# Block 0 of a streaming encoder layer: gate weights and a third conv tap inside the attention, two affine passes on ScalarE, a shorter inverse root

## The chip, the cores and the metric

The kernel runs on one core of one Trainium2 chip. A core has TensorE (PE in the profile: matrix products; its weight loads are shown as PEld), VectorE (DVE), ScalarE (ACT), GpSimd (POOL) and SyncE (SP, which only issues DMAs here). The metric is the device time of one execution in microseconds; a median of several runs is given. Lower is better.

## What is computed

One layer, on 2048 prompt frames and 32 sample frames of width 1024, all in float32:

```
mod = c @ w_mod + b_mod;  shift, scale, gate = split(mod, 3)
h = rms_norm(x, g_pre) * (1 + scale) + shift
a, b, z_conv, q, k, v, z_attn, g_conv, g_attn = split(h @ w_in)      # 512 wide, the last two 1024
u = a * sigmoid(b)
y = causal depthwise conv of u, 31 taps, + dw_b
y_conv = (silu(layer_norm(y)) * silu(z_conv)) @ w_conv_out
o = attention over the own 64-frame chunk and the 8 before it, 8 heads of 64, with a position bias
y_attn = (o * silu(z_attn)) @ w_attn_out
merged = sigmoid(g_conv) * y_conv + sigmoid(g_attn) * y_attn
out = x + gate * rms_norm(merged @ w_o, g_post)
```

The prompt and the sample frames have different conditioning vectors c, so `mod` has two rows. Caches of keys, values and conv inputs go in and out.

## The kernel before, in words

**Precision.** A float32 value is split into a high half (rounded to the type of fast matmuls, `F32R`) and a low half, the remainder. A product is three matmuls: high by high, high by low, low by high (`mm3`, line 257).

**Weights.** All weights of the program stand in one list, `plan` (lines 184 to 200), in the order of use. A call of `weights(key)` takes the next one. It also splits the weight two places ahead (`w_parts`, line 218: ACT rounds the high half, DVE or POOL subtracts), and issues the load of the one four places ahead (`w_load`). Raw weights have two buffers, split ones three. Each entry is 512 KB raw. Most weights are kept split in DRAM (`w_keep`, issued on ACT's queue) and read back by blocks 1 to 3; the gate's weights are used once. Which engine subtracts is chosen by line 227; inside block 0's attention it is POOL for all but gate weights, and in the tail of block 0 (`pace.dense`) it is DVE.

**Blocks and stages.** The frames go in four blocks of 512; block 0 also holds the 32 sample frames, so its projections run as two pieces of 272 columns. A block has these stages:
- value projection; in block 0 it is woven into the start (norm of x, first two thirds of `mod`, and `h`). `h_part` (line 334) makes `h` from a transposed piece: ACT writes the high half, DVE computes the same affine value again in full precision (`hf`), and DVE subtracts.
- attention: units (head pair, head, group of queries) with scores, exponentials, normalisation, transposes and the product with the values. Between these pieces `fill` issues pieces of other projections, in the order that `FILL(b)` gives: gated conv input (b, a), queries and keys of later head pairs, gates (z, c).
- tail: the two 1024-wide gates (`C_GC`, `C_GA`) and the attention branch's output, column by column; then the conv branch's output and the merge (line 1334 on), with `h` of the next block; then `w_o`, the next block's conv input, the post norm and the store.

**The conv** is 31 multiply-adds (taps) on each of 4 channel tiles, 128x574 in block 0, each one DVE instruction (`conv`, line 487). It is a generator that opens when the first channel tile of u is done. In the attention of block 0 it is advanced a fixed number of times at three places of a turn, by `TP`, in all turns but the last three (21 of 24). Otherwise, and in the whole tail, it is advanced when the planner's count for DVE has fallen behind. After the last tap comes `norm_conv` (mean and variance by matmul with a matrix of ones, the inverse root by `rsqrt` on 128x544, then POOL multiplies), and then `co` (line 1237), which makes swish and gate and splits the result into `cohi` and `colo`; the conv branch's product can't start before.

**The planner.** The order on PE, DVE, ACT and POOL is written by the program. `Pace` keeps two clocks, `pe` and `dve`, in estimated us: a matmul adds 6 + 0.4063 ns a column, a DVE instruction by its width (`Vec.call`, line 125). `pace.start(gen, delay)` runs a generator's pieces when `pe` has passed their due time. So `norm_conv`'s pieces are spaced by `YL` and `co`'s by 1.0. SP's queue is ordered by the framework's own scheduler. Three PSUM buffers (`pp`) serve all projections and short products; a projection's drain is issued late, at the next piece or at `pace.flush()`.

**The gate.** The last third of `mod` needs 8 weights (1024 rows by 1024 columns, as 256x512 pieces). Before, `gate_rows` in the tail took one of them after each column of the gates but the first, and the rest behind the last; `gate_row` adds the bias, multiplies by `g_post` and stores to DRAM (`gp_d`), from which the last stage reads it broadcast:

```
for m in (m2, m2 + 1):                       # tail, line 1298
    pace.run(proj(C_GC + m * P, b, ...))
    pace.run(proj(C_GA + m * P, b, ...))
    if gr and m:
        for i in range(2):
            next(gr, None)                   # four gate matmuls in two steps
            pace.tick()
```

Of the kernel before, what the change touches and what calls it, by code (L numbers as in the profile page):

```python
# [8 lines left out]
F32 = mybir.dt.float32  # L9
# [7 lines left out]
P = 128  # L17
D = 1024
# [16 lines left out]
NIN = 5632  # L35
BIG = 1e30
# [9 lines left out]
TP = (1, 1, 0)  # L46
# [5 lines left out]
def FILL(b):  # L52

    part = dict(q=C_Q, k=C_K, a=C_A, b=C_B, z=C_ZA, c=C_ZC)
# [84 lines left out]
def mixer_kernel(ctx, tc, x_prompt, x_sample, c_prompt, c_sample, cache_conv, cache_k, cache_v,  # L139
# [78 lines left out]
    def w_parts(i):  # L218

        if i < len(plan):  # L220
            key = plan[i][0]
            w = wp.tile([P, 2, 1024], F32R, tag="w", name="w", bufs=3)
            wh, wl = w[:, 0], w[:, 1]
            if i <= keep_at[key]:
                raw = raws.pop(i)
                act(wh, raw, AF.Copy)  # L226
                on_v = key[0] == "mod" or pace.dense or pace.idle is None and pace.dve <= pace.pe + DV
                (V if on_v else G).tensor_tensor(wl, raw, wh.bitcast(F32), op=OP.subtract)  # L228
            else:
                nc.sync.dma_start(w.bitcast(F32), kept[key])  # L230
            halves[i] = w
# [83 lines left out]
    def h_stats(pool, b, xs):  # L315

        xs += load_x(pool, b)
        yield 8.0
        ss = pool.tile([P, 8], F32, tag="ss", name="ss", bufs=2)
        V.memset(ss, 1.0)  # L320
        for t, (xt, m) in enumerate(xs):
            junk = ps.tile([P, 1024], F32, tag="S", name="junk")
            act(junk[0:m], xt[0:m], AF.Square, accum_out=ss[0:m, t:t + 1])
# [4 lines left out]
        V.tensor_scalar(ss, ss, 1.0 / D, EPS, op0=OP.mult, op1=OP.add)  # L328
# [152 lines left out]
    conv_ready, ln_done = set(), {}  # L481
# [78 lines left out]
    def mod_rows(n, dst):  # L560
        pm = ps.tile([P, 512], F32, tag="T", name="pm", bufs=2)
        for kp in range(KT // 2):
            wh, wl = weights(("mod", 2 * kp, n * 512))
            for kk in range(2):
                k = 2 * kp + kk
                mm(pm[0:4], c4[:, k, :], wh[:, kk, :], k == 0, False)
                mm(pm[0:4], c4[:, k, :], wl[:, kk, :], False, k == KT - 1)
                yield
        V.tensor_copy(dst, pm[0:4])

    def gate_rows(tmp):

        for n in range(2):
            m4, bg = tmp("m4")[0:4, 0:512], tmp("bg")
            bm, gr = bg[0:2, 0:512], bg[0:2, 512:1024]
            nc.sync.dma_start(bm, dram(b_mod, 2 * D + n * 512, [[0, 2], [1, 512]]))
            nc.sync.dma_start(gr, dram(g_post, n * 512, [[0, 2], [1, 512]]))
            yield from mod_rows(4 + n, m4)
            pace.start(gate_row(n, m4, bm, gr), 4.0)

    def gate_row(n, m4, bm, gr):
        pg = pp_tile("pg")
        nc.tensor.matmul(pg[0:2], lhsT=sel, rhs=m4, start=True, stop=True)
        V.tensor_tensor(bm, pg[0:2], bm, op=OP.add)
        V.tensor_tensor(bm, bm, gr, op=OP.mult)
        nc.sync.dma_start(gp_d[:, n * 512:(n + 1) * 512], bm)
        yield 0.0
# [31 lines left out]
    with tc.tile_pool(name="init", bufs=1) as ini:  # L619
# [64 lines left out]
        with tc.tile_pool(name="x0", bufs=5) as x0:  # L684
# [37 lines left out]
            V.tensor_scalar(ss, ss, 1.0 / D, EPS, op0=OP.mult, op1=OP.add)  # L722
# [74 lines left out]
    for b in range(NB):  # L797
# [5 lines left out]
        with tc.tile_pool(name="at", bufs=1) as at:  # L803
# [136 lines left out]
            def z_proj(col, dst, key):  # L940
                def sink(o, c0, c1):
                    tz = tmp("tz")
                    act(tz[:, c0:c1], o, AF.Tanh, scale=0.5)
                    V.scalar_tensor_tensor(dst[:, c0:c1], tz[:, c0:c1], 1.0, o, op0=OP.add, op1=OP.mult)
                def done():
# [5 lines left out]
                    C_B: lambda n: b_proj(b, n), C_A: lambda n: a_proj(b, n, tmp),  # L951
                    C_ZA: lambda n: z_proj(C_ZA + n * P, aof[:, n], ("za", n)),
# [225 lines left out]
            rate = (88.0 if b == 0 else 62.0) / sum(loads)  # L1178
# [50 lines left out]
        with tc.tile_pool(name="tl", bufs=1) as tl_:  # L1229
# [7 lines left out]
            def co():  # L1237
# [5 lines left out]
                def first(ct):  # L1243
                    xn[ct] = tl_.tile([P, NT], F32, tag="t1", name="xn", bufs=2)
                    th[ct] = tl_.tile([P, NT], F32, tag="hf", name="th", bufs=2)
                    for a0, a1, o0 in ypieces:
# [3 lines left out]
                        V.tensor_scalar(xn[ct][:, o0:o1], Y[ct][:, a0:a1], vecs[:, 44 + ct:45 + ct],  # L1250
                                        vecs[:, 48 + ct:49 + ct], op0=OP.mult, op1=OP.add)
# [42 lines left out]
            gr = gate_rows(lambda name: tl_.tile([P, D], F32, tag="x", name=name, bufs=XB)) if b == 0 else None  # L1294
            for m2 in range(0, KT, 2):
                if m2 == KT - 4 and b < NB - 1:
                    pace.start(h_stats(XP, b + 1, xs))
                for m in (m2, m2 + 1):
# [4 lines left out]
                    if gr and m:  # L1303
                        for i in range(2):
                            next(gr, None)
                            pace.tick()
# [59 lines left out]
            def gated(t, n):  # L1366
# [5 lines left out]
                act(jk[0:m], acc[t][0:m], AF.Square, accum_out=sq[0:m, n * 8 + t:n * 8 + t + 1])  # L1372
# [3 lines left out]
            def store(t0, t1, parts, apart=()):  # L1376
# [3 lines left out]
                V.tensor_scalar(rx[:, c], rx[:, c], 1.0 / D, EPS, op0=OP.mult, op1=OP.add)  # L1380
# [63 lines left out]
```

## Time and profile before

| | |
|---|---|
| median of 3 runs | 1776.56 us (1776.23 to 1776.82) |
| the profiled execution | 1774.66 us |
| its span, first to last instruction | 1772.9 us |
| mean granted TensorE clock | 0.982 |
| DVE busy | 1154.7 us (65%) |
| ACT busy | 597.5 us (34%) |
| POOL busy | 212.1 us (12%) |

Busy times are sums over the span. PE's matmuls are pipelined and their ends modelled, so a busy PE is not PE at its peak; idle time of PE is the surer reading. Block 0 takes about the first 632 us; blocks 1 and 2 some 400 each.

### The profile page before, as it was taken

What the parts mean: (1) busy time and instruction counts of PE and PEld (TensorE: products, weight loads), DVE (VectorE), ACT (ScalarE), POOL (GpSimd) and SP (SyncE); (2) the same over time, 40 slices, a digit from 0 to 9 for tenths busy, and PEclk for the clock granted to TensorE, in tenths of its full rate; (3) what the DMA queues carried; (4) which work ended last, traced back from release to release, by engine and by line L of the source; (5) the groups of instructions that cost most, each with busy time, mean ns of one, the idle gap of its engine ahead of it and who ended that gap; (6) DMA issues with size and microseconds to landing.
All of it is one profiled execution on the core that took longest, in us unless ns stands there. A gap on an engine that the chain in (4) does not pass through costs nothing.

```text
span 1772.9 us, 23618 instructions
## 1 busy us (share of the span) xinstructions
PE 1690.7 (95%) x9221; PEld 1430.4 (81%) x9221; DVE 1154.7 (65%) x2119; ACT 597.5 (34%) x1156; POOL 212.1 (12%) x163
## 2 busy tenths in 40 slices
PE   6889999989499999999899999999999999999997
PEld 4778899988388788888788888888888888888886
DVE  6556876887855957775652967765652967766523
ACT  5345454233331245531220035531320045531211
POOL 4322222002220000001120000001120000000120
PEclk9999999999699999999999999999999999999999
DMA  8796565767375684465465585455565574445553
GB/s 267 216 326 207 189 215 202 272 229 262 132 255 196 243 305 174 156 221 190 150 217 188 196 307 188 140 198 210 181 218 191 199 272 144 171 167 201 190 190 143
DMA packets 132326, 368.61 MB, mean 208 GB/s; under 512 B 9326, under 2 KB 75050, under 8 KB 101975
## 3 DMA queue, kind: packets, MB, share of 16 engines
q1 hardware_dynamic: 123575, 304.19, 50.1%
q10 hardware_dynamic: 8640, 62.92, 8.7%
q8 instruction: 73, 1.20, 0.3%
q14 instruction: 38, 0.31, 0.1%
HBM read 280.41 MB, written 91.77 MB: 210 GB/s over the span
## 4 chain that ended last, share of the span: by engine, by line
PE 78%; DVE 8%; DMA 4%; ACT 2%; issue 1%; ACTq 0%; POOL 0%; DVEq 0%; SPq 0%; POOLq 0%
PE pj L153 44%; PE py L153 8%; PE pv L153 4%; PE sps L153 4%; PE pt L157 4%; PE op L153 3%; PE oT L153 3%; PE oS L153 3%; PE oP L153 1%; DVE y L134 1%; DVE w L134 1%; PE vS L153 1%; PE vT L153 1%; DMA raw<-in_w_attn_out_dram 1%; DMA raw<-in_w_in_dram 1%
## 5 line engine op out<-in xcount | busy, mean ns | idle before, releaser
L153 PE MATMUL pj<-hh,w 128*128 128x512 f32 (+1 forms) x4800 | 974.7, 357 | 11.9 <-DVE kk L134 6.1
L153 PEld LDWEIGHTS pj<-hh,w 128*128 128x128 f32 x4800 | 778.4, 189 | 133.2 <-issue 8.9
L134 DVE SCALAR_TENSOR_TENSOR y<-u,dww,y 128x512 f32<-128x512 f32 (+1 forms) x480 | 338.2, 770 | 0.4
L1073 ACT ACTIVATE sp<-sp,mn 128x640 f32<-128x640 f32 (+5 forms) x136 | 103.7, 762 | 112.5 <-DVE mn L134 112.3
L1108 ACT ACTIVATE pth<-pt 128x256 fp32r<-128x256 f32 (+4 forms) x184 | 91.9, 501 | 135.8 <-PE pt L157 129.3
L134 DVE TENSOR_TENSOR ptl<-pt,pth 128x256 fp32r<-128x256 f32 (+4 forms) x184 | 104.2, 567 | 27.2 <-ACT pth L1108 25.4
L134 DVE CUSTOM_DVE_ANT_0 sp<-sps,bias 128x640 f32<-128x640 f32 (+4 forms) x128 | 94.4, 737 | 29.6 <-PE sps L153 28.1
L153 PE MATMUL py<-cohi,w 128*128 128x512 f32 (+1 forms) x320 | 93.5, 366 | 19.2 <-ACT cohi L1260 17.7
L226 ACT ACTIVATE w<-raw 128x1024 fp32r<-128x1024 f32 x72 | 75.6, 1054 | 89.1 <-DMA raw<-in_w_mod_dram 18.6
L153 PE MATMUL py<-ah,w 128*128 128x512 f32 (+1 forms) x480 | 96.3, 356 | 8.3 <-DVE t L134 7.1
L153 PEld LDWEIGHTS py<-ah,w 128*128 128x128 f32 x480 | 80.1, 192 | 23.5 <-DVE t L134 7.5
L157 PE MATMUL pt<-ident,sp 128*128 128x128 f32 (+1 forms) x600 | 94.2, 272 | 0.0
L228 POOL TENSOR_TENSOR w<-raw,w 128x1024 fp32r<-128x1024 f32 x30 | 73.3, 2443 | 170.5 <-ACT w L226 142.8
L528 POOL TENSOR_TENSOR u<-y 128x512 f32<-128x512 f32 (+1 forms) x4 | 6.3, 1581 | 671.4 <-DVE y L134 671.4
L153 PEld LDWEIGHTS py<-cohi,w 128*128 128x128 f32 x320 | 58.8, 195 | 29.0 <-ACT cohi L1260 19.1
L134 DVE TENSOR_SCALAR sp<-sp,ll 128x640 f32<-128x640 f32 (+5 forms) x136 | 75.6, 556 | 4.8
L134 DVE TENSOR_TENSOR w<-raw,w 128x1024 fp32r<-128x1024 f32 x42 | 53.3, 1278 | 31.5 <-ACT w L226 31.0
L153 PE MATMUL sps<-kk,qh 128*128 128x320 f32 (+1 forms) x224 | 69.2, 316 | 3.3 <-DVE kk L134 2.0
L157 PEld LDWEIGHTS pt<-ident,sp 128*128 128x128 f32 (+1 forms) x600 | 68.8, 140 | 3.9 <-issue 1.3
L153 PE MATMUL sps<-kk,ql 128*128 128x320 f32 (+1 forms) x224 | 70.8, 323 | 0.0
L1344 POOL TENSOR_TENSOR mg<-mg,t 128x512 f32<-128x512 f32 (+1 forms) x32 | 46.4, 1451 | 168.7 <-issue 114.0
L134 DVE SCALAR_TENSOR_TENSOR t<-t,py 128x512 f32<-128x512 f32 (+1 forms) x40 | 23.2, 584 | 59.3 <-PE py L153 59.2
(247 smaller groups left out, 2224.8 us busy)
## 6 DMA issues: line engine op xcount, KB each, us to landing
w<-kept SPq DMA_DIRECT2D x176, 1024.0 KB
kept<-w ACTq DMA_DIRECT2D x60, 1024.0 KB
raw<-in_w_in_dram SPq DMA_DIRECT2D x48, 512.0 KB
bias<-bias_d SPq DMA_DIRECT2D x32, 320.0 KB
xt<-in_x_prompt_dram SPq DMA_DIRECT2D x16, 512.0 KB
wm<-in_w_mod_dram SPq DMA_DIRECT2D x16, 512.0 KB
xr<-in_x_prompt_dram SPq DMA_DIRECT2D x16, 512.0 KB
vs_d<-vcur SPq DMA_DIRECT2D x12, 512.0 KB
```

Of the source, the lines that this page charges most:

```text
L134: return fn(out, *a, **k)
L153: nc.tensor.matmul(out, lhsT=lhsT, rhs=rhs, start=start, stop=stop)
L157: nc.tensor.transpose(out, in_, idn)
L226: act(wh, raw, AF.Copy)
L228: (V if on_v else G).tensor_tensor(wl, raw, wh.bitcast(F32), op=OP.subtract)
L528: G.tensor_tensor(s2[:, 0:YW], Y[2][:, 0:YW], Y[3][:, 0:YW], op=OP.add)
L1073: self.ex[i] = lambda: act(sp[0:m, 0:nk], sp[0:m, 0:nk], AF.Exp, bias=mn[0:m], scale=-1.0, accum_out=ll[0:m])
L1108: act(self.ph[0:r, f0:f1], pt[0:r, o:o + f1 - f0], AF.Copy)
L1344: G.tensor_tensor(mg, mg, t2, op=OP.add)
```

## The change

- `FILL(0)` gets eight pieces `m0` to `m7`, one gate weight each, woven between the projections from q1 to z0 (`C_MOD`, `mod_part`). The tail's `gate_rows` and `mod_rows` go, and `plan` follows. A gate weight's product now goes to a buffer of `pp`, and the sum over four weights is kept in SBUF: ACT copies the first, DVE adds the next three. Scratch for it is `aof`, before the attention gates are written there.
- The subtraction for the gate weights is no longer fixed to DVE: line 227 then gives it to POOL in the attention.
- `TP` goes from (1, 1, 0) to (1, 1, 1): a third tap a turn. The amount of filling a turn goes from 88 to 95.
- In `h_part` and `co` an affine pass moves from DVE to ACT (`hf`, `xn`), in all blocks.
- `rsqrt` has 9 instructions for 11: two steps, the second of higher order. The division by D moves into the squares before it.

```
-TP = (1, 1, 0)
+TP = (1, 1, 1)
-    order = "b0 a0 q1 k1 b1 a1 b2 q2 k2 a2 z0 b3 a3 z1 q3 k3 z2 z3 c0 c1 c2 c3" if b == 0 else \
+    order = "b0 a0 q1 m0 k1 m1 b1 m2 a1 m3 b2 q2 m4 k2 m5 a2 m6 z0 m7 b3 a3 z1 q3 k3 z2 z3 c0 c1 c2 c3" if b == 0 else \
...
+    def w_fill(n, col):
+        return w_wide("mod", w_mod, 2 * (n % 4), (4 + n // 4) * 512) if col == C_MOD else w_cols(col + n * P)
...
-                on_v = key[0] == "mod" or pace.dense or pace.idle is None and pace.dve <= pace.pe + DV
+                on_v = pace.dense or pace.idle is None and pace.dve <= pace.pe + DV
...
-    def rsqrt(y, x, xh, t, iters=3):
+    def rsqrt(y, x, t, u):
         V.tensor_scalar(y.bitcast(I32), x.bitcast(I32), -0.5, 1597463007.0, op0=OP.mult, op1=OP.add)
-        V.tensor_scalar(xh, x, -0.5, None, op0=OP.mult)
-        for _ in range(iters):
-            V.tensor_tensor(t, y, y, op=OP.mult)
-            V.tensor_tensor(t, t, xh, op=OP.mult)
-            V.scalar_tensor_tensor(y, t, 1.5, y, op0=OP.add, op1=OP.mult)
+        V.scalar_tensor_tensor(t, y, -0.5, y, op0=OP.mult, op1=OP.mult)
+        V.tensor_tensor(t, t, x, op=OP.mult)
+        V.scalar_tensor_tensor(y, t, 1.5, y, op0=OP.add, op1=OP.mult)
+        V.tensor_tensor(t, y, y, op=OP.mult)
+        V.tensor_tensor(t, t, x, op=OP.mult)
+        V.tensor_scalar(u, t, 0.375, -1.25, op0=OP.mult, op1=OP.add)
+        V.tensor_tensor(u, u, t, op=OP.mult)
+        V.scalar_tensor_tensor(y, u, 1.875, y, op0=OP.add, op1=OP.mult)
...
         act(hi, src, AF.Identity, scale=Gm[:, w, ct:ct + 1], bias=Sh[:, w, ct:ct + 1])
-        V.tensor_scalar(hf, src, Gm[:, w, ct:ct + 1], Sh[:, w, ct:ct + 1], op0=OP.mult, op1=OP.add)
+        act(hf, src, AF.Identity, scale=Gm[:, w, ct:ct + 1], bias=Sh[:, w, ct:ct + 1])
...
+    def mod_part(i):
+        n, kp = i // 4, i % 4
+        m4, bm, gr = aof[0:4, 3, 0:512], aof[0:2, 2, 0:512], aof[0:2, 1, 0:512]
+        if kp == 0:
+            nc.sync.dma_start(bm, dram(b_mod, 2 * D + n * 512, [[0, 2], [1, 512]]))
+            nc.sync.dma_start(gr, dram(g_post, n * 512, [[0, 2], [1, 512]]))
+        wh, wl = weights(("mod", 2 * kp, (4 + n) * 512))
+        pm = pp_tile("pm")
+        for kk in range(2):
+            mm(pm[0:4], c4[:, 2 * kp + kk, :], wh[:, kk, :], kk == 0, False)
+            mm(pm[0:4], c4[:, 2 * kp + kk, :], wl[:, kk, :], False, kk == 1)
+            yield
+        if kp == 0:
+            act(m4, pm[0:4], AF.Copy)
+        else:
+            V.tensor_tensor(m4, pm[0:4], m4, op=OP.add)
+        if kp == 3:
+            pace.start(gate_row(n, m4, bm, gr), 1.5)
...
-            rate = (88.0 if b == 0 else 62.0) / sum(loads)
+            rate = (95.0 if b == 0 else 62.0) / sum(loads)
...
-                        V.tensor_scalar(xn[ct][:, o0:o1], Y[ct][:, a0:a1], vecs[:, 44 + ct:45 + ct],
-                                        vecs[:, 48 + ct:49 + ct], op0=OP.mult, op1=OP.add)
+                        act(xn[ct][:, o0:o1], Y[ct][:, a0:a1], AF.Identity, scale=vecs[:, 44 + ct:45 + ct],
+                            bias=vecs[:, 48 + ct:49 + ct])
```

## Rows read from the trace of the kernel before

**Rows 1.** The page, engine lines: busy us, share of the span, instructions.
```profile
PE 1690.7 (95%) x9221; PEld 1430.4 (81%) x9221; DVE 1154.7 (65%) x2119; ACT 597.5 (34%) x1156; POOL 212.1 (12%) x163
```
**Rows 2.** Windows: length, busy us (instructions) by engine, granted clock, DMA share, GB/s.
```profile
core 0: us, PE busy (x) PEld busy (x) DVE busy (x) ACT busy (x) POOL busy (x), PEclk, DMA share, GB/s
...
126.00:206.00 80.00, 77.05 (x572) 67.96 (x570) 58.42 (x149) 42.58 (x103) 20.44 (x10) 1.00 0.57 195
206.00:300.30 94.30, 93.26 (x714) 85.39 (x714) 67.92 (x150) 44.22 (x106) 26.80 (x12) 1.00 0.58 205
300.30:442.20 141.90, 131.99 (x996) 125.62 (x996) 113.22 (x159) 48.40 (x78) 11.64 (x6) 0.98 0.73 254
442.20:473.00 30.80, 9.62 (x25) 4.82 (x23) 26.19 (x39) 9.41 (x16) 7.89 (x8) 0.56 0.32 110
473.00:504.00 31.00, 28.78 (x211) 27.70 (x212) 29.11 (x47) 14.03 (x26) 11.19 (x7) 0.95 0.60 213
...
1033.00:1432.00 399.00, 398.45 (x1962) 332.66 (x1961) 258.86 (x465) 122.15 (x236) 24.28 (x22) 1.00 0.57 203
```
**Rows 3.** Waits of PE, 100 to 660 us: total us, times, longest.
```profile
PE py L153 <- ACT cohi L1260: 17.7, 4, 13.8
...
PE py L153 <- DVE t L134: 7.1, 2, 6.2
```
**Rows 4.** The chain of waits, 300 to 660 us: start, length, what.
```profile
309.27 12.11 DMA raw<-in_w_attn_out_dram
...
329.31 6.95 DMA raw<-in_w_mod_dram
...
359.20 7.97 DMA raw<-in_w_in_dram
...
404.29 1.01 PE pg L583 x2
...
408.13 12.00 PE pj L153 x96
420.13 0.93 PE pm L153 x4
...
435.91 6.26 PE py L153 x48
...
476.45 0.44 PE pxt L157 x4
476.89 3.02 PE py L153 x24
...
500.70 3.26 PE py L153 x24
```
**Rows 5.** DVE groups by shape, 300 to 443 us: busy us, mean ns, idle before.
```profile
L134 DVE SCALAR_TENSOR_TENSOR y<-u,dww,y 128x574 f32<-128x574 f32 x80 | 60.8, 812 | 0.3
...
L134 DVE TENSOR_TENSOR bg<-pg,bg 2x512 f32<-2x512 f32 x1 | 0.7, 678 | 0.0
```
**Rows 6.** The conv's taps, 125 to 300 us: ns shortest/median/longest, first and last start.
```profile
L134 DVE SCALAR_TENSOR_TENSOR y<-u,dww,y x40: 795/808/3052, 131.7 to 297.6; 128x574 f32<-128x574 f32 x40
```
**Rows 7.** Timeline of DVE in the conv's root: start, length.
```profile
453.29 0.72 DVE L134 SCALAR_TENSOR_TENSOR u<-u 128x544 f32<-128x544 f32 x1
```
**Rows 8.** The tile hf, 0 to 600 us, columns as in rows 6.
```profile
L134 DVE TENSOR_SCALAR hf<-pxt,Gm,Sh x16: 798/805/814, 26.5 to 501.6; 128x512 f32<-128x512 f32 x16
```
**Rows 9.** The tile hh on ACT, whole span, columns as in rows 6.
```profile
L336 ACT ACTIVATE hh<-pxt,Sh,Gm x32: 759/778/781, 25.4 to 1317.6; 128x512 fp32r<-128x512 f32 x32
```
**Rows 10.** The tile raw, 125 to 210 us, columns as in rows 6.
```profile
L216 SPq DMA_DIRECT2D raw<-in_w_in_dram x9: 367/368/374, 131.0 to 209.0; - x9
```
**Rows 11.** Timeline, one weight on its way in attention: start, length.
```profile
154.81 1.06 ACT L226 ACTIVATE w<-raw 128x1024 fp32r<-128x1024 f32 x1 [0.39 <-PE pj L153]
...
156.01 2.38 POOL L228 TENSOR_TENSOR w<-raw,w 128x1024 fp32r<-128x1024 f32 x1 [6.56 <-ACT w L226]
...
158.41 0.37 SPq L216 DMA_DIRECT2D raw<-in_w_in_dram  x1
```
**Rows 12.** DVE groups by shape, 125 to 300 us, columns as in rows 5.
```profile
L134 DVE SCALAR_TENSOR_TENSOR y<-u,dww,y 128x574 f32<-128x574 f32 x40 | 36.2, 906 | 0.1
```

More of the change, by code (lines that the diff above doesn't have):

```diff
@@ L35 @@
 NIN = 5632
+C_MOD = -1
 BIG = 1e30
@@ L52, in FILL @@
 def FILL(b):
-    part = dict(q=C_Q, k=C_K, a=C_A, b=C_B, z=C_ZA, c=C_ZC)
-    order = "b0 a0 q1 k1 b1 a1 b2 q2 k2 a2 z0 b3 a3 z1 q3 k3 z2 z3 c0 c1 c2 c3" if b == 0 else \
+    part = dict(q=C_Q, k=C_K, a=C_A, b=C_B, z=C_ZA, c=C_ZC, m=C_MOD)
+    order = "b0 a0 q1 m0 k1 m1 b1 m2 a1 m3 b2 q2 m4 k2 m5 a2 m6 z0 m7 b3 a3 z1 q3 k3 z2 z3 c0 c1 c2 c3" if b == 0 else \
         "q1 k1 z0 q2 k2 z1 q3 k3 z2 z3 c0 c1 c2 c3"
@@ L182, in w_half @@
         return ((name, m), 2 * P, lambda r: (r, src[0, :, m * P:(m + 2) * P].rearrange("(k p) c -> p k c", p=P)))
-    mods = [w_wide("mod", w_mod, k, n * 512) for n in (4, 5) for k in range(0, KT, 2)]
+    def w_fill(n, col):
+        return w_wide("mod", w_mod, 2 * (n % 4), (4 + n // 4) * 512) if col == C_MOD else w_cols(col + n * P)
     for b in range(NB):
         plan += [w_wide("v", w_in, k, C_V) for k in range(0, KT, 2)]
-        plan += [w_cols(c + n * P) for n, c in [(0, C_Q), (0, C_K)] + FILL(b)]
+        plan += [w_fill(n, c) for n, c in [(0, C_Q), (0, C_K)] + FILL(b)]
         for m in range(0, KT, 2):
@@ L322, in h_stats @@
             junk = ps.tile([P, 1024], F32, tag="S", name="junk")
-            act(junk[0:m], xt[0:m], AF.Square, accum_out=ss[0:m, t:t + 1])
+            act(junk[0:m], xt[0:m], AF.Square, scale=D ** -0.5, accum_out=ss[0:m, t:t + 1])
             yield 2.0
@@ L327, in h_stats @@
         t2 = pool.tile([P, 8], F32, tag="ru", name="ru", bufs=2)
-        V.tensor_scalar(ss, ss, 1.0 / D, EPS, op0=OP.mult, op1=OP.add)
+        V.tensor_scalar(ss, ss, EPS, None, op0=OP.add)
         rsqrt(rr, ss, t1, t2)
@@ L478, in conv_rows @@
         nc.sync.dma_start(dst[0, 0], us[0:HIST, 0:512])
-    conv_ready, ln_done = set(), {}
+    conv_ready, ln_done, gate_done = set(), {}, set()
     def shape(b):
@@ L558, in norm_conv @@
         ln_done[b] = True
[L560 to L575, printed above, removed]
+    def mod_part(i):
+        n, kp = i // 4, i % 4
+        m4, bm, gr = aof[0:4, 3, 0:512], aof[0:2, 2, 0:512], aof[0:2, 1, 0:512]
+        if kp == 0:
             nc.sync.dma_start(bm, dram(b_mod, 2 * D + n * 512, [[0, 2], [1, 512]]))
             nc.sync.dma_start(gr, dram(g_post, n * 512, [[0, 2], [1, 512]]))
-            yield from mod_rows(4 + n, m4)
-            pace.start(gate_row(n, m4, bm, gr), 4.0)
+        wh, wl = weights(("mod", 2 * kp, (4 + n) * 512))
[10 more added lines that the diff above has]
+            pace.start(gate_row(n, m4, bm, gr), 1.5)
     def gate_row(n, m4, bm, gr):
@@ L583, in gate_row @@
         nc.tensor.matmul(pg[0:2], lhsT=sel, rhs=m4, start=True, stop=True)
+        yield 1.5
         V.tensor_tensor(bm, pg[0:2], bm, op=OP.add)
@@ L586, in gate_row @@
         nc.sync.dma_start(gp_d[:, n * 512:(n + 1) * 512], bm)
+        gate_done.add(n)
         yield 0.0
@@ L721, in mixer_kernel @@
             rr, t1, t2 = [x0.tile([P, 8], F32, tag=n, name=n, bufs=1) for n in ("rr", "rt", "ru")]
-            V.tensor_scalar(ss, ss, 1.0 / D, EPS, op0=OP.mult, op1=OP.add)
+            V.tensor_scalar(ss, ss, EPS, None, op0=OP.add)
             rsqrt(rr, ss, t1, t2)
@@ L941, in sink @@
                 def sink(o, c0, c1):
+                    assert len(gate_done) == 2 or key == ("za", 0)
                     tz = tmp("tz")
@@ L951, in mixer_kernel @@
                     C_B: lambda n: b_proj(b, n), C_A: lambda n: a_proj(b, n, tmp),
+                    C_MOD: mod_part,
                     C_ZA: lambda n: z_proj(C_ZA + n * P, aof[:, n], ("za", n)),
@@ L1293, in mixer_kernel @@
             xs = []
-            gr = gate_rows(lambda name: tl_.tile([P, D], F32, tag="x", name=name, bufs=XB)) if b == 0 else None
             for m2 in range(0, KT, 2):
@@ L1302, in mixer_kernel @@
                     pace.run(proj(C_GA + m * P, b, lambda o, c0, c1: act(t2[:, c0:c1], o, AF.Tanh, scale=0.5)))
[L1303 to L1306, printed above, removed]
                 wa = weights(("ao", m2))
@@ L1311, in mixer_kernel @@
                         t2[:, c0:c1], t2[:, c0:c1], 1.0, o, op0=OP.add, op1=OP.mult)))
-            if gr:
-                for _ in gr:
-                    pace.tick()
             while pace.idle is not None:
@@ L1379, in store @@
                 V.tensor_tensor(rx[:, c], sq[:, t0:t1], sq[:, 8 + t0:8 + t1], op=OP.add)
[L1380 removed]
+                V.tensor_scalar(rx[:, c], rx[:, c], EPS, None, op0=OP.add)
                 rsqrt(ry[:, c], rx[:, c], rz[:, c], rw[:, c])
```

10 lines of the change are left out of this document (3 added, 7 removed).

## The prediction

> **What bounds the kernel now.** I read the page's engine lines first: TensorE (PE) is busy 1690.7 us, 95% of the span [rows 1]. The reader is to see from this only that time can come from places where PE is idle. The table by stage says where those are [rows 2]. From 1033 to 1432 us, all of block 2, PE is busy 398.45 of 399 us: the change can't gain there and needs only to do no harm. Block 0 is different. Its attention (126 to 300.3) leaves PE idle 2.95 and 1.04 us. Its tail leaves 9.9 us up to 442.2, then 21.2 of 30.8 us up to 473, then 2.2 us up to 504. So 33.3 us of idle PE lie in 203.7 us. In the worst stretch the mean granted clock is 0.56, so most of it ran at 1.2 instead of 2.4 GHz.
>
> The waits of PE name two causes [rows 3]: 17.7 us for cohi, the first product of the conv's end, and 7.1 us for t, the drain of the attention branch. The chain of waits shows where the second comes from: raw weights landing after 6.95 to 12.11 us, their split on ScalarE (ACT) and VectorE (DVE), and conv taps queued on DVE between two splits [rows 4]. The first wait is the same shortage later on: 80 of the 120 accumulating taps are still to do when attention ends, 60.8 us of DVE [rows 5, 6]; only after the last can mean, variance, root and swish follow. The tail is bound by DVE and by weight supply, attention by PE.
>
> **The change part by part.** Units: a projection of block 0 is 48 matmuls, 6.0 us (12.00 for 96); an attention-output weight 6.26; a gate weight 0.93; a gate row's matmul 1.01; one conv-output column 3.02 to 3.26 and its transposes 0.44 [rows 4].
>
> *Tail after.* PE work left in it: 16 projections, 96.0; 4 attention-output weights, 25.0; the means' matmuls, some 0.8; 8 conv-output columns of 3.14 + 0.44, 28.6. That is 150.4 us against 203.7 now. The difference of 53.3 us is the gate's matmuls and rows, the 33.3 us of idle time, and the rest (some 10 us) matmuls that now run at the low clock. How much idle stays?
> - Weight supply. Two raw buffers, so one round trip serves two weights: landing 7 to 8 us, 1.05 ACT, some 1.2 DVE, and a tap or two in front on DVE, 10.9 to 12. Without gate weights the tail uses a weight every 6.1 us, 12.2 for two, where it used one every 5.1. It just fits, except at the start, where the next block's x loads make one landing 12.11 [rows 4]. I leave 4 us (bounds 1 and 9.9, today's idle).
> - The wait for cohi. Attention issues two taps in each of its first 21 turns. The trace has 40 accumulating taps there, from 131.7 to 297.6 [rows 6], and the first ones of two channel tiles: two in each of 19 turns, since the conv opens only in the third, and 4 in idle moments. So 19 turns gain one, and of 124 taps 63 are left instead of 82. In the tail the planner issues a tap whenever its count for DVE has room, so the planned end of the taps follows from its own costs (code, not trace). A column of the tail is 13.98 planned us of PE (two projections of 5.59, half an attention-output weight 2.80), eight are 112; each holds 2.5 splits of 1.135 and two drains of 0.42 on DVE, 26%. 63 taps of 0.733 are 46, branch input, x scaling and root 8: (46 + 8)/0.74 = 73. Norm and swish are spaced over 31 + 10 planned us, so they end at 114, some 2 after the last branch matmul. Two root steps fewer (0.72 each [rows 7]) and the normalised value on ACT shorten it. I leave 3 us (bounds 0 and 17.7).
> - The conv-output stage keeps 2 of 2.2 us; there 8 h values leave DVE (0.805 each) for ACT (0.778 each) [rows 8, 9].
>
> 159.4 against 203.7: minus 44.3 us.
>
> *Attention.* It has almost no idle PE, so moved matmuls cost their whole length: 8 x 0.93 + 2 x 1.01 = 9.5 us. Around them I put 5 us of new idle time, from:
> - Weight supply. A weight comes every 9.76 us in the early stretch (nine loads from 131.0 to 209.0 [rows 10]). 6.0 of that is projection, 3.8 attention. With 8% more filling per turn (95 for 88) the second part falls to 3.5; a gate weight adds 0.93 + 0.5. A pair takes 10.9 us for two weights. The loop: a split starts on ACT at 154.81, GpSimd (POOL) starts its part at 156.01, the next load is issued at 158.41 [rows 11], 3.6 later; with a landing of 7 that is 10.6 for two weights. It fits by 0.3 us. The gate's b_mod and g_post loads and the gp_d store now stand on SP's queue among the raw loads; the store waits for two DVE operations, and the raw load behind it with it. 2 us (bounds 0 and 39, see the rivals).
> - PSUM. Each gate weight takes one of three buffers that the projections rotate through, so the next projection may wait for a drain behind ACT's queue. PE's idle 2.95 us in the early stretch [rows 2], in which other tiles already cut in, bounds it below 3; 1.5.
> - DVE. 19 taps of 0.906, 6 additions and 4 operations of the gate rows, each near the 2x512 addition's 0.68 [rows 5, 12]: 24 us on 126.3 of 174.3 busy [rows 2], so 150 of 184. It hides behind the filling; 1.5 (bounds 0 and 12). The two copies to SBUF are on ACT, busy half the time: nothing, at most 2 x 0.78.
>
> Plus 14.5.
>
> *The rest.* Before attention 8 wide h values move to ACT; chains there mix both engines and loads. Between a gain of 3 (half of 8 x 0.805 saved) and a loss of 2 I take -0.5. In blocks 1 to 3 the same moves fall where PE has no gap [rows 2]; ACT is busy 122 of 399, and next to it 24 times 0.778 and the 12 normalised values disappear. Nothing; if the lower half came late at each column, 0.8 us each. Root steps on 8 columns and moving 1/D into the squares: under 1 us together, not counted.
>
> **Sum.** -44.3 + 14.5 - 0.5 = -30.3 us. The profiled execution took 1774.66, so 1744.4; the median of the runs is 1.9 above it: 1746.3.
>
> **The rivals.**
> *All hides.* Idle 2 instead of 9 in the tail, none new in attention, 3 gained before it: 14.5 better, 1731.8. For it: the supply fits on paper in both stages. Against: it fits by tenths, and the present tail lost 9.9 us in such a state.
> *The conv wait stays.* The taps come earlier but the chain behind them doesn't, and PE still waits 17.7 instead of 3: 1761.0. For it: by the sum above the chain ends just where the branch does. Against: the same sum for today, with 82 taps, puts the last tap at 103 of 119 planned us, so the room behind it grows from 16 to 39.
> *DVE becomes the bound in attention.* In the stretch with the gate weights (80 us, now 58.4 of DVE) the pairs take 87; 63.5 + 11 taps of 0.906 + 6.8 is 80, 92%. The rows show a tap of 3.052 where the median is 0.808, and all 40 together, 36.2 us, cost 3.9 over the median, 0.23 for each of some 17 weights that POOL splits meanwhile at one in 9.76 us [rows 6, 10, 12]; with 8 more splits that is 1.8 us and still fits. If instead each split cost DVE its whole 2.38 us [rows 11], 19 us come on top, 99 in 87, and attention is 12 longer: 1758.3. Such a case is what the Trainium skill, "SBUF — State Buffer", section "SBUF: two separate sides", would have: GpSimd and a VectorE operation with two SBUF inputs share an exclusive port pair, held for the whole instruction. The longest tap agrees with it; the sum of the 40 says the collision is rare.
> *Slower.* The weight loop in attention. If raw weights land after 12.11 us there, as once in the tail when loads collide [rows 4], two weights take 15.7 instead of 10.9: 4.8 x 8 = 39, and against the 2 counted that is 37 worse, 1783. It decides from a landing of some 11 us. For it: 0.5 MB more every 10.9 us beside bias loads and kept weights. Against: DMA is 57% busy there, and the tail at 73% had 7 to 8 [rows 2, 4].
>
> **Chances and range.** Forecast 0.52, all hides 0.13, the conv wait 0.14, DVE 0.13, slower 0.05, unforeseen 0.03. Conv wait and DVE together would give 1773, at the edge of what can be told from no change (0.2%, 3.5 us): I take 0.04 of them there and 0.01 of the slower case. Faster 0.88, same 0.05, slower 0.07. The range goes from 1733, near the floor that the first rival gives, to 1768, past either middle rival alone; it leaves out half of the first, and above it the middle two's sum, the slower case and the unforeseen: some 0.18.
>
> **What would show it.** Right: no PE wait for cohi above some 4 us, the tail near 160 us, attention some 15 us longer, and about 19 taps more before it ends. Wrong: ACT's split of a gate weight waiting on its load (supply); a PE wait of 10 us or more for cohi (conv); PE waiting in attention on drains or maxima with DVE above 90% (DVE). A change outside block 0 above 3 us would refute the part on the rest.

## The result and the profile after

The changed kernel took 1757.63 us (median of 4 runs, 1755.64 to 1762.16) against 1776.69 for the kernel before (1776.23 to 1778.99): a ratio of 0.9894, 95% interval 0.9872 to 0.9915. The forecast was 1746.3, range 1733 to 1768. So the kernel gained 19 us where 30 were forecast.

The page's engine line of after answers to [rows 1]:

```profile
PE 1687.3 (96%) x9221; PEld 1429.5 (81%) x9221; DVE 1121.9 (64%) x2030; ACT 634.3 (36%) x1218; POOL 232.1 (13%) x170
```

The totals hardly move. The windows show what moved, cut at the end of each kernel's stages (the last attention output, then the first product of each block's `w_o`): attention of block 0, its tail, block 1. Columns are as in [rows 2]. The kernel before, in these cuts:

```profile
115.50:300.10 184.60, 180.61 (x1363) 162.92 (x1362) 132.63 (x316) 92.80 (x223) 49.78 (x24) 1.00 0.60 207
300.10:503.80 203.70, 170.40 (x1230) 158.11 (x1231) 168.32 (x244) 71.65 (x117) 30.71 (x21) 0.91 0.65 226
503.80:920.70 416.90, 408.98 (x1990) 338.29 (x1989) 272.49 (x482) 133.95 (x252) 27.83 (x30) 0.99 0.58 207
```

The same three stages after:

```profile
116.00:332.10 216.10, 197.85 (x1398) 171.78 (x1397) 166.20 (x347) 101.08 (x233) 71.81 (x32) 0.96 0.58 197
332.10:493.60 161.50, 153.07 (x1194) 151.09 (x1195) 130.66 (x190) 72.98 (x126) 30.62 (x21) 0.99 0.72 258
493.60:904.80 411.20, 405.93 (x1990) 336.42 (x1990) 263.74 (x464) 142.42 (x265) 27.99 (x30) 1.00 0.59 211
```

The first number behind the two times is the length, the next PE's busy time; their difference is idle PE. The tail became 42.2 us shorter (idle 33.3 to 8.4) where 44.3 were forecast. Block 1 became 5.7 shorter. Attention became 31.5 longer, where 14.5 were forecast. Its idle PE went from 4.0 to 18.3, and PE's own busy time grew by 17.2. The moved matmuls are 9.5 of that by the forecast's units; the other 7.7 go with a clock that fell: the granted clock, 1.00 before, was at 1.2 GHz for 17.1 us after. 14.3 + 9.5 + 7.7 = 31.5. The start (115.5 to 116.0), block 2 (399.4 both) and the end (-0.7) did nothing.

PE's waits in the attention after (total us, times, longest):

```profile
PE pj L155 <- DVE kk L136: 4.0, 1, 4.0
PE pg L587 <- DVE aof L136: 3.5, 1, 3.5
PE sa L155 <- DVE mn L136: 2.4, 2, 1.4
PE pj L155 <- ACT u L446: 2.0, 1, 2.0
PE pm L155 <- DVE ql L136: 1.6, 1, 1.6
PE po L159 <- DVE aof L136: 1.6, 1, 1.6
PE pj L155 <- DVE aof L136: 1.0, 1, 1.0
```

And in the tail after, where [rows 3] had 17.7 us for cohi:

```profile
PE py L155 <- DVE t L136: 4.5, 2, 2.9
PE py L155 <- ACT t L1309: 2.2, 2, 1.2
PE py L155 <- DVE mg L136: 1.5, 3, 0.6
```

No wait for cohi is left. The longest wait that is left, 2.9 us for t, still comes from a weight that landed late; the chain of after in the tail:

```profile
350.31 10.87 DMA raw<-in_w_in_dram
...
362.35 1.22 DVE w L136
363.57 0.36 DVE t L136
...
363.98 2.68 PE py L155 x12
```

The drain t stands on DVE behind the split of that weight. The other waits for t (423.1, 458.7 and 462.0 us, 3.8 in all) fall beside the passes of the norm and the swish on ACT.

Why cohi is ready in time is seen from the tile of the taps: after has 60 accumulating taps in attention, where [rows 6] had 40, with the same columns. The last tap of block 0 is at 406.7 us instead of 420.7.

```profile
L136 DVE SCALAR_TENSOR_TENSOR y<-u,dww,y x60: 795/808/2901, 128.1 to 325.0; 128x574 f32<-128x574 f32 x60
```

The largest new wait, in the timeline of after (start, length, what):

```profile
138.17 1.09 PE L155 MATMUL pm<-w,c 128*4 128x512 f32 x4
...
139.98 0.80 DVE L136 SCALAR_TENSOR_TENSOR y<-u,dww,y 128x574 f32<-128x574 f32 x1
...
140.47 1.04 ACT L226 ACTIVATE w<-raw 128x1024 fp32r<-128x1024 f32 x1
...
141.43 0.80 DVE L136 SCALAR_TENSOR_TENSOR y<-u,dww,y 128x574 f32<-128x574 f32 x1
142.26 1.81 DVE L136 TENSOR_TENSOR kk<-pj,kk 64x272 fp32r<-64x272 f32 x4
```

The gate weight `m1` had just been multiplied. The drain of the key projection before it was issued only behind that, as the rule "at the next piece" has it, and so behind a weight's split on ACT and taps on DVE. The next projection needed its buffer and stood for 4.03 us, up to 143.30. The windows from the end of that wait on and one equal stretch later:

```profile
142.60:149.40 6.80, 6.10 (x27) 5.83 (x28) 6.68 (x11) 3.08 (x7) 4.30 (x2) 0.50 0.87 318
149.40:156.20 6.80, 6.80 (x49) 5.74 (x50) 4.64 (x13) 1.93 (x6) 0.00 (x0) 1.00 0.36 102
```

A granted clock of 0.50 and 27 matmuls (the first 0.7 us are still the wait), then 1.00 and 49: the wait is paid twice. The second large wait, at 231.7 us, is of another kind:

```profile
228.71 5.16 POOL L228 TENSOR_TENSOR w<-raw,w 128x1024 fp32r<-128x1024 f32 x2 [4.24 <-ACT w L226]
...
231.60 2.89 DVE L136 SCALAR_TENSOR_TENSOR y<-u,dww,y 128x574 f32<-128x574 f32 x1
...
234.41 0.67 DVE L136 TENSOR_TENSOR aof<-pm,aof 4x512 f32<-4x512 f32 x1
...
235.13 1.86 PE L587 MATMUL pg<-aof,sel 4*2 4x512 f32 x2 [3.45 <-DVE aof L136]
```

The gate row's matmul is due 1.5 planned us behind the last gate weight, but its operand `aof` is added on DVE behind a tap, and this tap took 2.89 us beside POOL's splits of two projection weights. Again 6.8 us at 0.50 follow (234.8 to 241.6).

### The profile page after: what moved, and what is told of

It is laid out like the page before. It is cut to its first block, busy times and chain, and to the rows that moved or that the text cites. A ratio compares the mean times of both kernels' runs of the same rounds, so it can differ in the third digit from the quotient of the medians.

```text
span 1756.3 us, 23599 instructions
## 1 busy us (share of the span) xinstructions
PE 1687.3 (96%) x9221; PEld 1429.5 (81%) x9221; DVE 1121.9 (64%) x2030; ACT 634.3 (36%) x1218; POOL 232.1 (13%) x170
## 4 chain that ended last, share of the span: by engine, by line
PE 82%; DVE 7%; DMA 4%; ACT 3%; issue 2%; POOL 1%; SPq 0%; ACTq 0%; POOLq 0%; DVEq 0%
PE pj L155 46%; PE py L155 9%; PE pv L155 4%; PE sps L155 4%; PE pt L159 4%; PE op L155 3%; PE oT L155 3%; PE oS L155 3%; PE vS L155 2%; PE vT L155 2%; DVE sp L136 2%; DMA raw<-in_w_in_dram 1%; PE oP L155 1%; DVE y L136 1%; DMA bias_d<-lrow_d 1%
## 5 line engine op out<-in xcount | busy, mean ns | idle before, releaser
L136 DVE SCALAR_TENSOR_TENSOR y<-u,dww,y 128x512 f32<-128x512 f32 (+1 forms) x480 | 345.5, 781 | 0.5
L228 POOL TENSOR_TENSOR w<-raw,w 128x1024 fp32r<-128x1024 f32 x37 | 92.2, 2497 | 191.9 <-ACT w L226 169.8
L226 ACT ACTIVATE w<-raw 128x1024 fp32r<-128x1024 f32 x72 | 75.7, 1052 | 70.8 <-DMA raw<-in_w_in_dram 17.1
L136 DVE TENSOR_SCALAR sp<-sp,ll 128x640 f32<-128x640 f32 (+5 forms) x136 | 84.4, 621 | 4.8
L1308 ACT ACTIVATE t<-pj 128x512 f32<-128x512 f32 (+1 forms) x40 | 20.7, 517 | 128.3 <-PE pj L155 128.1
L136 DVE SCALAR_TENSOR_TENSOR t<-t,py 128x512 f32<-128x512 f32 (+1 forms) x40 | 23.2, 584 | 67.1 <-PE py L155 67.0
```

Source lines behind the costliest of these rows:

```text
L136: return fn(out, *a, **k)
L1308: pace.run(proj(C_GC + m * P, b, lambda o, c0, c1: act(t1[:, c0:c1], o, AF.Tanh, scale=0.5)))
```

## The experiments

Each kernel ran in five rounds beside the kernel before (medians of it 1777.3, 1777.9, 1777.3 and 1777.6 in the four groups). The table has the medians, the ratio with its interval, and from each profile the attention with its idle PE and its time at 1.2 GHz, and the tail with its idle PE; all in us.

| kernel | median | ratio | attention (idle, 1.2 GHz) | tail (idle) |
|---|---|---|---|---|
| before | 1776.69 | 1 | 184.6 (4.0, 0) | 203.7 (33.3) |
| after | 1757.63 | 0.9872 to 0.9915 | 216.1 (18.3, 17.1) | 161.5 (8.4) |
| e1 two taps | 1769.71 | 0.9952 to 0.9980 | 207.0 (12.6, 6.8) | 182.8 (23.2) |
| e2 flush first | 1753.03 | 0.9854 to 0.9891 | 211.9 (15.4, 13.7) | 161.5 (8.4) |
| e3 split on DVE | 1771.58 | 0.9963 to 0.9983 | 220.3 (19.2, 23.9) | 164.7 (10.3) |
| e4 gate in the tail | 1754.89 | 0.9867 to 0.9904 | 189.1 (6.9, 3.4) | 188.2 (17.8) |
| e5 the rest only | 1769.98 | 0.9940 to 0.9973 | 185.7 (4.5, 0) | 206.9 (32.6) |
| e6 old root | 1765.24 | 0.9919 to 0.9945 | 216.4 (18.2, 17.1) | 164.4 (8.3) |
| e7 no gate split | 1755.90 | 0.9866 to 0.9894 | 218.5 (15.8, 27.3) | 159.8 (7.9) |
| e8 gate spread | 1766.15 | 0.9918 to 0.9945 | 215.8 (18.3, 17.1) | 167.3 (11.2) |
| e9 gate in the tail on POOL | 1758.88 | 0.9892 to 0.9923 | 189.7 (7.0, 3.4) | 192.2 (21.9) |
| e10 flush, later row | **1746.08** | 0.9816 to 0.9856 | 206.7 (11.8, 10.2) | 159.9 (8.2) |
| e11 gate late | 1764.88 | 0.9922 to 0.9948 | 221.0 (17.8, 27.3) | 164.7 (9.3) |
| e12 late taps | 1759.66 | 0.9874 to 0.9912 | 217.3 (18.1, 17.1) | 163.8 (9.3) |

A caution for reading it: the start, which only e6 touches, took 112.4 to 117.9 us in the thirteen profiles with the changed front, with 6.8 to 17.1 us of it at 1.2 GHz. One profile is uncertain by some us for that alone. Idle time and named waits repeat better. The kernels stand in four groups, so small differences between medians of different groups say little.

### Which part earns what: e1, e4, e5, e6

e1 takes the third tap out, all else stays:

```
-TP = (1, 1, 1)
+TP = (1, 1, 0)
```

> The changed kernel with TP back at (1, 1, 0): two taps a turn, all else as changed (median 1757.6 us). Theory D (VectorE is late in the attention because of the taps, the gate's additions and collisions with GpSimd's splits): attention's idle PE falls from 18.3 us to about 10 and the half-clock spells shrink, some 12 us gained there; but 82 taps instead of 62 are left for the tail, its conv ends some 18 us later and PE waits for cohi again: 1761 to 1767. Theory B (the gate weight takes one of three projection buffers, and the drain of the next one is issued late): attention as in the changed kernel within 2 us, tail 16 to 18 us longer: 1772 to 1776.

It lost 12.1 of the 19 us and lies between the two ranges. The waits of its tail hold the wait for cohi again (12.8 at its longest), with the last tap at 422.5 us:

```profile
PE py L155 <- ACT cohi L1268: 16.7, 4, 12.8
```

Attention was 9.1 shorter without the third tap, with 12.6 us of idle PE instead of 18.3, the tail 21.3 longer. So the early taps remove the conv wait, and they have a price of their own in the attention, which the forecast put at 1.5.

e4 puts the gate back: `FILL(0)`, `plan`, `mod_rows`, `gate_rows`, the rate of 88 and the split on DVE are those of before; the third tap, the passes on ACT and the short root stay.

> The changed kernel with the gate's weights back in the tail (order, filling and split as before), third tap, affine passes on ScalarE and the shorter root kept. The 20 taps moved forward bring the conv's end some 20 us forward; the shorter root keeps its gain of 5.5 us in block 1. Theory D: the taps alone cost attention 3 to 6 us (VectorE 78% to 86% busy): 1754 to 1758. Theory B: attention within 2 us of the kernel before: 1750 to 1754. In both, much of the gain is there without moving the gate.

1754.89, in theory D's range, against 1757.63, with intervals that overlap. Its attention and tail are

```profile
115.90:305.00 189.10, 182.22 (x1363) 164.49 (x1361) 147.72 (x335) 92.47 (x222) 51.57 (x24) 0.99 0.58 202
305.00:493.20 188.20, 170.42 (x1229) 160.51 (x1230) 144.10 (x204) 80.36 (x133) 29.12 (x21) 0.95 0.71 245
```

Against after, attention is 27.0 shorter and the tail 26.7 longer, with `w_o` of block 0 starting at 493.2 instead of 493.6. The move of the gate, the first item of the change, here only carried time from one stage to the other. The third tap alone costs attention 3.4 here (189.1 against 185.7 in e5); beside the gate weights it cost 9.1.

e5 is e4 with `TP = (1, 1, 0)`: what is left of the change is the passes on ACT and the root.

> The kernel before with the affine passes on ScalarE and the shorter root alone: two taps a turn, the gate in the tail. Root theory: 5.5 us in block 1 and some 1.5 in block 0's conv end, the affine passes 1 to 3 in block 0's tail: 1768 to 1771. If the third tap and the gate's move simply add up, it is 1769.7 + 1754.9 - 1757.6 = 1767. Rival (the 5.5 us of block 1 came from the new timing, not from the root): 1774 to 1776.

1769.98, in the root theory's range and 7.9 under the kernel before in the same group. e1, e4, e5 and after make a square: the third tap is worth 15.1 us with the gate in the tail and 12.1 with it in attention; the gate's move 0.3 gained without the tap and 2.7 lost with it, neither of them clear of the intervals.

e6 is after with the eleven instructions of the old `rsqrt`.

> The changed kernel (1757.6 us) with the inverse root of before, 11 instructions. Root theory: in block 1 the root on 8 columns again holds the drain of the attention branch behind it on VectorE while GpSimd multiplies, so PE waits over 4 us there and falls to the low clock, and block 0's conv end is 1.5 us later: 1763 to 1766. Rival (block 1 gained by other timing): 1758 to 1760.

It lost 7.6, in the root theory's range. That is nearly all of e5's 7.9, so the passes on ACT are worth nothing that can be told from intervals of some 3 us. In block 1 PE waits 4.5 us for the drain t in e6, as in before; in after it waits 2.4. The end of the root and what follows, DVE, POOL and PE in before:

```profile
860.38 5.07 POOL L556 TENSOR_TENSOR y<-y,u 128x512 f32<-128x512 f32 x4 [18.30 <-DVE ss L134]
...
861.74 1.22 DVE L134 TENSOR_TENSOR ru<-rr 128x8 f32<-128x8 f32 x1
...
865.51 0.17 DVE L134 TENSOR_TENSOR ru<-rr 128x8 f32<-128x8 f32 x1
...
869.37 1.28 DVE L134 SCALAR_TENSOR_TENSOR t<-t,py 128x512 f32<-128x512 f32 x2
...
870.11 2.50 PE L153 MATMUL pj<-hh,w 128*128 128x512 f32 x5 [4.48 <-DVE t L134]
```

The same place in after:

```profile
847.29 5.06 POOL L560 TENSOR_TENSOR y<-y,u 128x512 f32<-128x512 f32 x4 [17.11 <-DVE ss L136]
...
848.65 1.21 DVE L136 SCALAR_TENSOR_TENSOR rt<-rr 128x8 f32<-128x8 f32 x1
...
852.41 0.17 DVE L136 TENSOR_TENSOR rt<-rr 128x8 f32<-128x8 f32 x1
...
856.07 1.28 DVE L136 SCALAR_TENSOR_TENSOR t<-t,py 128x512 f32<-128x512 f32 x2
```

The drain t stands on DVE behind the conv's wide root, the 8-column root of the x rows and the x scaling. The 8-column root is hardly shorter (860.22 to 866.68 before, 847.13 to 853.39 after, 6.46 and 6.26 us). The wide root is: its last operation starts 0.3 us ahead of PE's last 24 projection matmuls in before (859.61 and 859.88), 2.2 ahead in after (846.52 and 848.68). Those 1.9 us are nearly all of the 2.1 by which the wait for t fell. In e6, with the long root again, they are 0.3 (853.09 and 853.36) and the wait is 4.5. Idle PE in block 1 was 7.9 in before and 7.6 in e6, and 5.3 to 5.5 in every kernel with the short root. The rest of block 1's change is clock: the same code with the short root took 411.2 to 414.3 us in twelve profiles, with 0 to 6.8 us of it at 1.2 GHz. Of the 7.6 us by the medians, only 2.3 are shown as idle time. By the profiles 5.2 of e6's loss lie in block 1 and 2.9 in the tail, where idle PE is the same (8.3 and 8.4) and 10.2 us instead of 3.4 ran at 1.2 GHz.

### The order of issue in the attention: e2, e10

e2 issues the pending drain before the gate weight:

```
     n, kp = i // 4, i % 4
+    pace.flush()
```

> The changed kernel with the pending drains of the projections issued before each gate weight. Theory B: the waits of PE on drains in the attention (some 12 of 18 us) mostly go, about 10 us gained with the half-clock spells: 1746 to 1750. Theory D: drains come earlier in VectorE's order but it is as loaded as before: within 3 us of 1757.6.

1753.03, between the two ranges. The waits for kk, ql and aof ahead of `pj` and `pm`, 7.0 us in after, are down to 0.4; attention is 4.2 shorter, since other waits grew:

```profile
PE sa L155 <- DVE mn L136: 5.4, 2, 3.3
PE pg L588 <- DVE aof L136: 3.5, 2, 2.2
```

The ratio's interval overlaps that of after, so its gain alone is shown by the waits rather than by the time: the waits went as theory B had it, less than half of its 10 us came. e10 adds a later due time for the gate row's matmul:

```
-            pace.start(gate_row(n, m4, bm, gr), 1.5)
+            pace.start(gate_row(n, m4, bm, gr), 6.0)
```

> The kernel with drains issued first (1753.0 us), and the gate row's matmul due 6.0 planned us after the last addition instead of 1.5. Its two waits on that addition were 1.25 and 2.23 us. If such a wait is simply lost time, 3.5 us and a half-clock spell go: 1747 to 1750. If VectorE is the queue behind all of them and another wait takes its place, as after the earlier drains: 1751 to 1755.

1746.08, 11.5 under after and with an interval clear of it (against e2 the intervals just touch): the best version. It is also 8.8 under e4, clear of it: with the two lines the move of the gate does pay. That it meets the forecast of 1746.3 is luck in part, since attention is still 22.1 longer than before, not 14.5, and block 1 gave 5.5 that were not counted. Its attention and tail:

```profile
114.50:321.20 206.70, 195.00 (x1398) 169.36 (x1398) 170.84 (x350) 101.87 (x235) 72.28 (x32) 0.98 0.61 207
321.20:481.10 159.90, 151.74 (x1193) 149.53 (x1194) 130.51 (x190) 72.88 (x125) 29.50 (x21) 1.00 0.73 261
```

The waits for `pg` are gone. Left in the attention are

```profile
PE sa L155 <- DVE mn L136: 5.2, 2, 3.3
PE sps L155 <- DVE kk L136: 2.4, 1, 2.4
```

So 9.4 of the attention's excess, by the profiles, came from two places in the program's order, in which a matmul or a drain was issued without regard to what DVE had queued.

### What the rest of the idle time is: e3, e7, e8, e9, e11, e12

*Collisions of POOL's splits with DVE.* In the attention of after, DVE's instructions took 18.6 us more, added up, than the median of their operation, tiles and shape in the whole run, and 9.9 before (the 19.7 in the texts below goes by medians in the attention alone). e3 has the gate's splits on DVE again, in the attention:

```
-                on_v = pace.dense or ...
+                on_v = key[0] == "mod" or pace.dense or ...
```

> The changed kernel with the gate weights' low halves subtracted on VectorE (1.23 us each) instead of GpSimd (2.4 us). Theory D with collisions as the main part: VectorE's time over the usual lengths falls from 19.7 to about 10 us in the attention against 9.8 us of added splits, its longest blocked instructions go, and attention gets 2 to 6 us shorter: 1752 to 1756. Theory D with plain load as the main part, or theory B: no change within 2 us, 1756 to 1760.

It was 14 slower than after, which neither side had expected; 7.4 of it lie in attention and tail by the profiles, most of the rest in the start and block 1, whose code is the same. e7 takes the gate's part of that work away altogether: the gate weights' low halves are not computed, and the high half is multiplied in their place, so the gate values are not the reference's. PE's work is the same.

```
+                if key[0] != "mod":
                     (V if on_v else G).tensor_tensor(wl, raw, ...)
...
-            mm(pm[0:4], c4[...], wl[:, kk, :], False, kk == 1)
+            mm(pm[0:4], c4[...], wh[:, kk, :], False, kk == 1)
```

> The changed kernel with the gate weights' low halves not computed; the second matmul of a pair uses the high half again, so TensorE has the same work but the gate is less exact. Theory C (what hurts attention are eight more GpSimd subtractions, each blocking VectorE's instructions): VectorE's time over the usual lengths falls from 19.7 to about 10 us, idle PE in attention from 18.3 to 10 or less: 1746 to 1749. Rival (density: a weight's ScalarE pass, additions, buffers and DMA crowd the projections that follow it): within 3 us of 1757.6.

1755.90, the same as after within the intervals and inside the rival's range, with DVE still 17.7 over its median lengths:

```profile
113.60:332.10 218.50, 202.70 (x1398) 176.05 (x1397) 160.27 (x347) 101.03 (x233) 54.55 (x25) 0.94 0.57 195
```

POOL lost 17.3 us of work and PE 2.5 us of idle time, and the low clock (27.3 us) took that back. The two long waits are the same, 4.4 and 3.45 us, and so is the tap of 2.89 us ahead of the second: the split beside it is a projection weight's. So the gate's splits are not the main cause. The 25 instructions that POOL still runs there are not tested by this. But in e2 and e10 the time over the median lengths is higher than in after, 24.0 and 25.1, and attention is shorter; so that sum doesn't set the attention's length.

*Too many gate weights in a short stretch.* e8 is e2 with the gate weights spread over all the filling, one in every 1.75 projections:

```
+    order = "b0 a0 q1 m0 k1 b1 m1 a1 m2 b2 q2 m3 k2 a2 m4 z0 b3 m5 a3 m6 q3 m7 k3 z1 z2 ..."
```

> The kernel with drains issued first (1753.0 us), and the gate weights spread to one in 1.75 projections (q1 m0 k1 b1 m1 a1 m2 b2 q2 m3 k2 a2 m4 z0 b3 m5 a3 m6 q3 m7 k3 z1) instead of one behind each from q1 to z0. Density theory: two raw weights split back to back make VectorE late; at half the density idle PE in attention falls from 15.4 to about 9 us and half-clock spells from 13.7 to about 5: 1743 to 1747. Theory C (each split costs the same wherever it stands): 1751 to 1755.

13 slower than e2, outside both ranges. By the profiles 3.9 us of it lie in attention, where idle PE rose from 15.4 to 18.3 instead of falling to 9, and 5.8 in the tail. Density alone is not it.

*The wrong place.* e11 is e2 with the gate behind `k3`, late in the attention. Its scratch is `zcb`, and the second half's rows overwrite the first's, so its gate values are not the reference's; the operations are the same. The gate row is due 1.0 instead of 1.5 planned us behind.

```
+    order = "b0 a0 q1 k1 b1 a1 b2 q2 k2 a2 z0 b3 a3 z1 q3 k3 m0 z2 m1 m2 z3 m3 m4 c0 m5 m6 m7 c1 c2 c3"
+        m4, bm, gr = zcb[0:4, 3, 0:512], zcb[0:2, 2, 0:512], zcb[0:2, 1, 0:512]
```

> The kernel with drains issued first, the gate weights placed after k3 (k3 m0 z2 m1 m2 z3 m3 m4 c0 m5 m6 m7 c1), where attention leaves PE idle only about 1% and VectorE is 70 to 74% busy; scratch in zcb instead of aof. If the place in the early stretch is what hurts (new keys, cached keys and taps all on VectorE there): attention 9.5 + 2 to 6 us longer than with the gate in the tail, 1738 to 1745. If any gate weight in the attention costs over twice its PE time wherever it stands: 1750 to 1757.

1764.88, 12 slower than e2 and outside both ranges. The waits of the early stretch shrank, but late in the attention PE now waited 3.9 us for DVE (osm), 1.9 for a gate row and for POOL's splits themselves (1.0 to 1.3 us three times), with 27.3 us at the low clock.

*Taps crowding DVE early.* e12 is e10 with the third tap moved to the later turns:

```
-                    pace.pump(int(TP[2]))
+                    pace.pump(2 if n >= 9 else 0)
```

> The kernel with drains issued first and the gate row later (1746.1 us), and the third taps moved: none in the first 9 turns, where the gate's weights stand, two in each of the next 12 (24 instead of 19). If VectorE's load in that early stretch is what still makes PE wait there for maxima and keys (3.3, 1.9 and 2.4 us, with 10.2 us at the low clock): these waits halve, attention is 4 to 8 us shorter, and the tail has 5 taps fewer: 1737 to 1742. If the waits come from the order alone, or the late turns can't hold two more taps: 1745 to 1751.

With no third tap in the first nine turns and two extra in the later ones it was 13.6 slower than e10, outside both ranges, and the waits are no fewer:

```profile
PE sa L155 <- DVE mn L136: 5.1, 3, 2.8
PE sps L155 <- DVE mn L136: 3.7, 4, 2.7
PE po L159 <- DVE osm L136: 2.8, 3, 1.1
```

*The gate in the tail with less DVE work.* e9 is e4 with the gate's splits on POOL there:

```
+                on_v = key[0] != "mod" and pace.dense or ...
```

> The gate in the tail with the third tap (1754.9 us), its weights' low halves subtracted on GpSimd instead of VectorE. Its tail still leaves PE idle 15.8 us up to cohi, with 20.5 us at the low clock. If VectorE's load sets that tail, 8 x 1.23 us less of it: 1745 to 1750. If the weight loop or GpSimd's own norm work does: a split takes 2.4 instead of 1.2 us in the loop, 1754 to 1760.

4 slower than e4, in the rival's range, though the intervals overlap. PE waits longer, for drains on DVE:

```profile
PE py L155 <- DVE t L136: 11.3, 3, 6.0
PE pg L589 <- DVE t L136: 5.9, 1, 5.9
```

With seven splits fewer DVE was busy 150.0 us in the tail instead of 144.1, and its time over the median lengths went from 5.8 to 17.3. So here POOL's splits held up DVE's own work by more than they took off it, which is another mechanism than the weight loop that the rival named first.

What stays open: why the 11.8 us of idle time and the 10.2 at 1.2 GHz in e10's attention remain. No edit aimed at the gate's splits, the density, the place or the early taps made the attention shorter; what the projections' splits on POOL cost it no run tells. The waits name single moments in which the maxima (mn) or a key's drain (kk) were late on DVE. That they come from the fixed order of DVE's queue, like the two that e2 and e10 removed, is argued and not shown.

## Why the prediction was right in direction and off in size

**The tail: right.** -42.2 against -44.3, idle 8.4 against 9. Supply, counted 4, is the wait of 2.9 behind the weight that took 10.87 us to land, at the start as forecast. The wait for cohi, counted 3, is gone, but the end of the conv still shows in 3.8 us of waits for the drains t beside norm and swish. The conv-output stage, counted 2, has 1.5 for mg. e1 shows that the third tap made the wait go, as argued. It also shows whose gain it was: the tail's 42 us hold some 24 to 27 that the gate's move brought, and attention gave nearly all of these back, 21.3 without the tap (e5, e1) and 27.0 with it (e4, after).

**Attention: the step that failed.** "Around them I put 5 us of new idle time" against 14.3. By its terms: supply, counted 2, was nothing: no wait of ACT for a raw weight is in the trace there. The rival of the weight loop fell with it. PSUM, counted 1.5 and bounded "below 3" by the idle time of before, was 7.0: that bound was taken from an order in which only short tiles cut in between two projections, and didn't hold for an order in which the drain itself is issued behind the newcomer. DVE, counted 1.5, was the rest, the wait for the gate row (3.5) in front. The term left out is the clock: I charged a wait at its own length, and each of the two long ones was followed by 6.8 us at 1.2 GHz. They are 13.6 of the 17.1 us that cost the 7.7.

**The third tap's price.** It was hidden behind PE in the sum. e1 has it at 9.1 us beside the gate weights; without them it is 3.4. Each addition to DVE alone was cheap and both together were not.

**The rest: refuted by its own test.** A change outside block 0 above 3 us was to refute it, and block 1 changed by 5.7. "In blocks 1 to 3 the same moves fall where PE has no gap" rested on block 2's row [rows 2] and was not looked up for block 1, where PE waited 4.5 us for t. The root there, "under 1 us together, not counted", is on DVE behind the conv's wide root, and the shorter root together is worth 2.3 us of idle time in block 1, and 7.6 in all by e6's medians. The affine moves at nothing agree with e5 and e6, as far as their intervals tell.

**The rivals.** Their times say little here. "DVE becomes the bound" gave 1758.3, nearly what was measured, by a price of 19 us for POOL's splits; e7 took the gate's splits away and gained 1.7. Of its test, PE waiting on drains and maxima, half came true; but DVE was busy 166 of 216 us, 77%, and 80% from 128 to 240 us, where the gate weights are, not above 90%. It was late, not full. That the time came near this rival's is luck.

## What to carry to other kernels

When work is woven into a stage where the critical engine has no gaps, count besides its length every result that it leaves pending: what is issued ahead of that drain on its engine, and who needs the buffer next; then look for those waits in the trace first: two lines of issue order brought 11.5 us here, over a third of what the whole change was to bring. A move between two stages brings only what the stage that takes the work doesn't give back in waits: the gate's move freed 24 to 27 us in the tail and cost 21 to 27 in the attention, with the third tap and without it, and paid (8.8 us, e10 against e4) only once the two lines were in. Look at the waits of every block before an edit in all blocks is put at nothing.

## What the runs showed of the hardware

- Small DVE instructions beside POOL are dear. In the root's fences, 128x8 operations take 0.17 us, but four of them took 1.21 to 1.28 while POOL ran four multiplies in 5.06 us, one POOL instruction's length (1.27) each. A tap with a median of 0.81 us took 2.89 within a stretch of POOL's splits. The Trainium skill, "SBUF — State Buffer", section "SBUF: two separate sides", says that whichever of the two comes first holds the shared ports for its whole instruction; these rows agree. What this is worth in all depends on the stage: without eight of POOL's splits, those of the gate, the kernel gained 1.7 us, within its interval (e7); with seven more of them in the tail, DVE's time over its median lengths there rose by 11.5 us (e4, e9).
- PE's waits of 4.03 and 3.45 us in after's attention were each followed by 6.8 us at 1.2 GHz, the one of 2.9 in its tail by 3.4, and the one of 2.4 in its block 1 by none. In the start and block 1 the same code spent 6.8 to 17.1 and 0 to 6.8 us at that level in different profiles.
